# Where two blocks of tokens are scaled and stored: a hybrid decoder layer on one core

## The chip, the cores and the metric

One core of a Trainium2 chip runs the whole kernel. The metric is the device time of one execution in microseconds; the profile is one further execution, recorded instruction by instruction on the same program. TensorE is called PE, VectorE DVE, ScalarE ACT, GpSimd POOL and SyncE SP in all tables.

## The reference, cut to what matters

One decoder layer over 4096 new tokens and 64 sample tokens. Only its first half is concerned here: the normalised tokens times one projection, whose columns are then given to a convolution, a windowed attention and a cross-attention.

```python
def _rmsnorm(x, g):
    xf = x.astype(jnp.float32)
    r = lax.rsqrt(jnp.mean(xf * xf, axis=-1, keepdims=True) + RMS_EPS)
    return (xf * r).astype(x.dtype) * g

def _layer(x, ...):
    h = _rmsnorm(x, g_pre)          # 1024 features
    z = h @ w_in                    # 22 column tiles of 128
    cb, cc, ch, cg, q, k, v, ag, mq, mg = _split_cols(z)
    ...
    y = jnp.concatenate([out_a, out_b, out_c], axis=-1) @ w_out
    return x + _rmsnorm(y, g_post), new_conv, new_k, new_v
```

## The kernel before, in words

**Tiles and phases.** The 4160 tokens are cut into 8 blocks of 520; a block is four tiles `B11`, `B21`, `B12`, `B22` of 128 partitions x 4 x 260 (feature half by token half). The 22 column tiles of the weight are done in three phases over all blocks: in the names of the code and here phase 0, 1 and 2 (the short title's "phase 1" and "phase 2" are phases 0 and 1). Every operand is split into a high and a low part (`split`, line 273 on ACT and 274 on DVE), and a product is three matmuls per k (`product`, line 283). Most blocks use Strassen's seven products (`PRODUCTS`); the operands T1 to T4 are differences of the four tiles (`t_sum`, line 266). One product on four column tiles is a "step" of 48 matmuls.

**The two plain blocks.** Phase 0 begins with blocks 0 and 1 done with eight plain products each (`plain_block`), since the Strassen sums of the weights are not there yet. What is done beside each step is written out by hand in `plain_jobs` and `plain_loads`. All of phase 0 is issued in program order on every engine (`manual_schedule`); phases 1 and 2 are ordered by the scheduler. In the plain blocks the row factors of the norm are not applied to x but afterwards to the result z (`z_rows`, line 527).

**Row factors.** `row_load` loads 104 token rows (tile `nat`, two buffers, line 207) on SP; `row_step` squares and sums them on ACT (line 218). After five of these POOL computes the factors (lines 222 and 223) and stores them to the DRAM tensor `rowd` (line 224). `row_queue` puts the collected row loads on SP and, two calls later, the load that spreads `rowd` over all partitions (tile `rb`, two buffers, line 234). SP works its queue in order, so whatever waits there holds up all that stands behind it.

**Tokens for phases 1 and 2.** In phase 0 each x tile is loaded from `in_xt` (line 188), multiplied by the gain on ACT (line 246) and by its row factor on DVE (line 254; line 252 for block 0, with the gain), and stored to the DRAM tensor `hd` through POOL's queue (line 127). For the plain blocks the split needs only the gain, or no more than x itself in block 0 (line 491), so their scaled copies are made for later phases alone. Phase 1 loads x from `hd` (line 442).

**Other names.** `temp` is a ring of 6 buffers in phase 0; the results of a finished block (`finish`: `th`, `v`, `zh`, `kl_`) are made in it, and each of its buffers is free once the store of its last user has landed. `flush` hands the collected stores to the queue at the next step. `o_kn`, `o_kc`, `o_vc` (lines 1129 to 1131), the loads of `us` (line 366) and of `gmem` (line 626) are copies with no fixed place, which the scheduler has put early in SP's queue, between the loads of the plain blocks.

Of the kernel before, what the change touches and what calls it, by code (L numbers as in the profile page):

```python
# [8 lines left out]
F32 = mybir.dt.float32  # L9
# [3 lines left out]
ALU = mybir.AluOpType  # L13
AX = mybir.AxisListType

P = 128
# [35 lines left out]
def hybrid_layer(ctx: ExitStack, tc: tile.TileContext, a: dict):  # L52
# [38 lines left out]

    def open_phase(ph):
        nonlocal tp, zp, natp, pa2, pa1
        tp = own.enter_context(tc.tile_pool(name=f"t{ph}", bufs=(6, 9, 4)[ph]))
        if ph == 0:
            natp = own.enter_context(tc.tile_pool(name="nat", bufs=2))
        zp = own.enter_context(tc.tile_pool(name=f"z{ph}", bufs=(5, 7, 3)[ph]))
        if ph != 1:

            psa.close()  # L100
            pa2 = psa.enter_context(tc.tile_pool(name=f"pa{ph}", bufs=2, space=bass.MemoryType.PSUM))
            if ph == 2:
                pa1 = psa.enter_context(tc.tile_pool(name="pa1", bufs=1, space=bass.MemoryType.PSUM))
# [76 lines left out]
    def x_load(b, o):  # L180

        kh, g0 = int(o[1]) - 1, (2 * b + int(o[2]) - 1) * HW
        t = hxp.tile([P, KH, HW], F32, tag="hx", name=f"x{b}{o}")
        g = g0
        while g < g0 + HW:
            src, off, n = (a["xt0"], g, 320) if g < 320 else (a["xt"][(g - 320) // 384], (g - 320) % 384, 384)
            w = min(n - off, g0 + HW - g)
            DMA.dma_start(t[:, :, g - g0 : g - g0 + w], src[:, KH * kh : KH * kh + KH, off : off + w])
            g += w
        return t  # L190

    RG = 104

    rows = []
    nat, sq = {}, [0]

    row_loads, row_spreads = [], {}

    def row_load(j):
        if j < 5 * NBLK:  # L200
# [26 lines left out]
    def row_queue():  # L227

        for j in row_loads:
            row_load(j)  # L230
        row_loads.clear()
        for b in [b for b, n in row_spreads.items() if n == 1]:
            rows.append(natp.tile([P, 2 * HW], F32, tag="rb", name=f"rb{b}"))
            DMA.dma_start(rows[b], rowd[b].partition_broadcast(P))
        for b in list(row_spreads):
            row_spreads[b] -= 1
            if row_spreads[b] == 0:
                del row_spreads[b]
# [8 lines left out]

    def scale(x, b, o):
        rb = rows[b][:, HW * (int(o[2]) - 1) : HW * int(o[2])]
        if b == 0:  # L250
            for k in range(KH):
                V.scalar_tensor_tensor(x[:, k], x[:, k], gain_of(o, k), rb, op0=ALU.mult, op1=ALU.mult)
        else:
            V.tensor_tensor(x, x, rb.unsqueeze(1).to_broadcast([P, KH, HW]), op=ALU.mult)
        store(hd[b][o], x)

    def t_sum(ph, b, o):

# [98 lines left out]
    def finish_conv(b, ct, zc, zh, zg, zb):  # L357
        zc, zh, zg, zb = (flat(z) for z in (zc, zh, zg, zb))
        n = 2 * HW
        ns = NS if b == 0 else 0  # L360
        m = n - ns
        V.scalar_tensor_tensor(zg, zb, 0.5, zg, op0=ALU.mult, op1=ALU.mult)
        ub = temp(f"ub{b}_{ct}")[:, : 2 + m]
        if ns:
            us = tiny.tile([P, NB, 10], F32, tag="us", name=f"us{ct}", bufs=2)
            DMA.dma_start(us[:, :, 0:2], a["convst"][ct])
            V.memset(ub[:, 0:2], 0.0)
            V.tensor_tensor(us[:, :, 2:10], zc[:, :ns].rearrange("p (b t) -> p b t", b=NB),
                            zh[:, :ns].rearrange("p (b t) -> p b t", b=NB), op=ALU.mult)
# [61 lines left out]
    def h_split(i):  # L431
        if i < len(steps):
            ph, b, p = steps[i]
            o = PRODUCTS[p][1]
            hs[i] = split(xs[ph, b][o], f"{ph}_{b}{o}")

    def x_of(ph, b, o):
        if ph == 0:
            t = x_load(b, o)
        else:  # L440
            t = hxp.tile([P, KH, HW], F32, tag="hx", name=f"x{ph}_{b}{o}")
            DMA.dma_start(t, hd[b][o])
        xs.setdefault((ph, b), {})[o] = t

    def x_gain(b, o):
        gain(xs[0, b][o], o)

    def x_scale(b, o):
        scale(xs[0, b][o], b, o)

    def x_ready(ph, b, o):
        if ph == 0:
            x_gain(b, o)
            x_scale(b, o)

    def next_block(ph, b, p):

# [7 lines left out]
            jobs = [load(o) for o in jobs]  # L465
        if p < 3:
            jobs.append(lambda: t_sum(ph, b, f"T{p + 2}"))
        if ph == 0 and (1 <= p < 6 or (b, p) == (PLAIN_BLOCKS, 0)):
            jobs.append(row_step)
        if nph < 2:  # L470
            jobs += [ready(o) for o in {4: "B11", 5: "B21 B12", 6: "B22"}.get(p, "").split()]
            if p == 6:
                jobs.append(lambda: t_sum(nph, nb, "T1"))
        return jobs

# [3 lines left out]

    def x_split(b, o):
        x = xs[0, b][o]
        if b > 0:
            h0[b, o] = split(x, f"0_{b}{o}")
            return
        h0[b, o] = hi, lo = [hp.tile([P, KH, HW], F32R, tag=n, name=f"{n}0_{b}{o}") for n in ("hi", "lo")]
        for k in range(KH):
            g = gain_of(o, k)  # L490
# [38 lines left out]

    def plain_jobs(b, s):  # L530

        gains = lambda b, *os: [lambda o=o: x_gain(b, o) for o in os]
        scales = lambda b, *os: [lambda o=o: x_scale(b, o) for o in os]
        parts = lambda b, o: [lambda: x_split(b, o)]
        fill = lambda o: [lambda q=q: first_fill(o, q) for q in range(4)]
        sums = lambda q, k: [lambda: first_sums(q, k)]
# [9 lines left out]
            (0, 5): lambda: [*sums(1, 0), *gains(1, "B11"), *sums(1, 1), *fills(1, "S2"), *row, *fills(1, "S3")],  # L546
            (0, 6): lambda: [*parts(1, "B11"), *fills(1, "S1", "S4"), *row, *sums(3, 0), *gains(1, "B21")],
            (0, 7): lambda: [*fills(3, "S2", "S3"), *row, *fills(3, "S1")],
            (1, 0): lambda: [*parts(1, "B21"), *scales(0, "B11", "B21"), *row, *z_rows(0, 1), *row],
            (1, 1): lambda: [*z_rows(0, 0), *done(0, 1), *row, *row],  # L550
            (1, 2): lambda: [*scales(0, "B12", "B22"), *done(0, 0), *row, *gains(1, "B12"), *row],
            (1, 3): lambda: [*parts(1, "B12"), *sums(2, 0), *gains(1, "B22"), *row],
            (1, 4): lambda: [*sums(2, 1), *fills(2, "S2"), *scales(1, "B11"), *row, *scales(1, "B21")],
            (1, 5): lambda: [*parts(1, "B22"), *gains(2, "B11"), *fills(2, "S3"), *row, *fills(2, "S1", "S4"), *gains(2, "B21")],
            (1, 6): lambda: [*scales(1, "B12", "B22"), *row, *scales(2, "B11", "B21")],
            (1, 7): lambda: [lambda: h_split(0), *gains(2, "B12"), *scales(2, "B12"), lambda: t_sum(0, 2, "T1"), *row,
                             *gains(2, "B22"), *scales(2, "B22"), *z_rows(1, 1)],
        }[b, s]()

    def plain_loads(b, s):  # L560
        for o in {(0, 0): ["A22"], (0, 1): ["A12"]}.get((b, s), ()):
            first_w(o)
        if (b, s) == (0, 0):
            row_load(0)
            row_load(1)
        row_queue()
        for nb, o in {(0, 1): [(0, "B12")], (0, 2): [(0, "B22")], (0, 4): [(1, "B11")], (0, 5): [(1, "B21")],
                      (1, 2): [(1, "B12"), (1, "B22")], (1, 4): [(2, "B11"), (2, "B21")],
                      (1, 6): [(2, "B12"), (2, "B22")]}.get((b, s), ()):
            x_of(0, nb, o)  # L570

    def plain_block(b):
        banks, zz[b] = {}, [[None, None], [None, None]]
# [45 lines left out]
    def third_start():  # L619
# [3 lines left out]
        third["pre"] = pre_stack.enter_context(tc.tile_pool(name="pre", bufs=1, side="right"))  # L623
        third["mem"] = mem_stack.enter_context(tc.tile_pool(name="mem", bufs=3, side="right"))
        third["ps"] = psa.enter_context(tc.tile_pool(name="psm", bufs=2, space=bass.MemoryType.PSUM))
        DMA.dma_start(gmem, a["gmem"])

    def mem_load(k):
        xm = third["mem"].tile([P, 256], F32, tag="xm", name=f"xm{k}")
# [70 lines left out]
    def input_projection():  # L700
        raws = {}
        for i, (ph, b, p) in enumerate(steps):
# [14 lines left out]
            h_load(i + 3)  # L717
            h_split(i + 1)
            jobs = list(pending.pop(i, ()))
            if ph == 0:  # L720
                row_queue()
            if ph < 2:
                jobs += next_block(ph, b, p)
            if ph == 2:
# [336 lines left out]
    def sample_window(sp):  # L1061
# [61 lines left out]
        for j in range(4):  # L1123
            for kvh in range(2):
# [1 line left out]
                c0 = (kvh * 4 + j) * 8  # L1126
                V.scalar_tensor_tensor(mix_s[r, 4 + j, :].rearrange("p (b t) -> p b t", b=NB), o3[r, :, c0 : c0 + 8], 0.5,
                                       zs[r, 6 + j, :].rearrange("p (b t) -> p b t", b=NB), op0=ALU.mult, op1=ALU.mult)
        DMA.dma_start(a["o_kn"], zs[:, 4:6, :])
        tc.keep_in_program_order(DMA.dma_start(a["o_kc"], a["cwk_nat"]))  # L1130
        tc.keep_in_program_order(DMA.dma_start(a["o_vc"], a["cwv_nat"]))
        yield
# [257 lines left out]
```

## Time and profile before

| | us |
|---|---|
| median of three runs | 1694.85 (1692.13 to 1697.65) |
| the profiled execution, whole | 1707.98 |
| its span | 1706.3 |
| PE busy / DVE busy / ACT busy / POOL busy | 1594.1 / 1183.9 / 784.2 / 358.5 |
| phase 0 on PE, first matmul to the first of phase 1 | 8.87 to 404.39 |

The profiled execution is 13.1 us longer than the median run. Busy time of PE is not time at full speed: the clock that it is granted falls to 0.5 in places, and a mean of 0.965 is recorded over the span. Instruction lists give start, duration, engine, line, operation with output and inputs, and in brackets how long the engine had stood idle and what released it. The lists of waits give total, number and longest.

### The profile page before, as it was taken

How to read it: one execution, taken by the hardware profiler on the slowest of the kernel's cores; microseconds unless marked ns; L12 is line 12 of the kernel's file. 1: busy time of each engine (PE TensorE's matmuls, PEld its weight loads, DVE VectorE, ACT ScalarE, POOL GpSimd, SP SyncE). 2: the span in 40 equal slices, each digit the busy share in tenths (PEclk: the TensorE clock that was granted, in tenths of full speed). 3: DMA queues.
4: the chain of work that ended last, by engine and by line, in shares of the span. 5: the costliest groups of instructions: out<-in, count | busy, mean ns of one | idle time of the engine just before them, and what ended most of it. 6: DMA issues, size and time to landing. Idle time of an engine off the chain costs nothing.

```text
span 1706.3 us, 29560 instructions
## 1 busy us (share of the span) xinstructions
PE 1594.1 (93%) x11073; PEld 1409.8 (83%) x11073; DVE 1183.9 (69%) x2113; ACT 784.2 (46%) x2000; POOL 358.5 (21%) x595
## 2 busy tenths in 40 slices
PE   7856999998999999979999975999999999999998
PEld 7856999998999999979999963677777777777766
DVE  6736777788788777965666656677677766767743
ACT  6544555555222222434443435555555555555521
POOL 0312222221000000000000014444443344333320
PEclk9977999999999999999999987999999999999989
DMA  7798899967565333669775769676677776666151
GB/s 215 148 261 214 213 243 251 252 235 272 135 214 176 127 114 115 217 171 272 252 249 197 255 176 193 126 151 141 140 143 156 156 160 133 136 151 135 50 182 62
DMA packets 170228, 306.69 MB, mean 180 GB/s; under 512 B 29030, under 2 KB 98406, under 8 KB 170054
## 3 DMA queue, kind: packets, MB, share of 16 engines
q1 hardware_dynamic: 123157, 226.21, 43.3%
q0 software_dynamic: 46928, 78.59, 23.7%
q8 instruction: 88, 1.44, 0.4%
q14 instruction: 55, 0.44, 0.1%
HBM read 196.54 MB, written 109.19 MB: 179 GB/s over the span
## 4 chain that ended last, share of the span: by engine, by line
PE 48%; DVE 19%; DMA 10%; issue 9%; ACT 8%; POOL 5%; SPq 0%; ACTq 0%; POOLq 0%; DVEq 0%
PE c L283 36%; PE y L1213 6%; ACT sm L954 5%; DVE sm L960 3%; DMA md<-th 2%; DVE sm L944 2%; DVE wmx L946 2%; DMA wor<-in_w_out 2%; POOL xp L909 2%; DVE yn L1220 1%; PE wt L964 1%; PE xs L901 1%; DVE xr L1231 1%; DVE mix L928 1%; ACT xp L905 1%
## 5 line engine op out<-in xcount | busy, mean ns | idle before, releaser
L1213 PE MATMUL y<-wo,mh 128*128 128x512 f32 (+1 forms) x1072 | 351.8, 392 | 1.4 <-DVE mh L1190 1.4
L290 DVE TENSOR_TENSOR z<-c,z 128x520 f32<-128x520 f32 (+1 forms) x308 | 195.0, 646 | 105.5 <-PE c L283 99.9
L1213 PEld LDWEIGHTS y<-wo,mh 128*128 128x128 f32 x1072 | 201.1, 189 | 42.1 <-issue 2.8
L1213 PE MATMUL y<-wo,ml 128*128 128x512 f32 (+1 forms) x520 | 202.8, 390 | 0.0
L954 ACT ACTIVATE sm<-sm,wnm 128x128 f32<-128x128 f32 x256 | 99.9, 391 | 76.1 <-DVE wnm L948 76.1
L1213 PEld LDWEIGHTS y<-wo,ml 128*128 128x128 f32 x520 | 98.4, 189 | 15.3
L941 PE MATMUL ws<-kst,q 128*128 128x256 f32 x512 | 82.3, 303 | 8.6 <-ACT sm L943 5.9
L971 POOL TENSOR_SCALAR_AFFINE_SELECT wpv<-wpt 128x512 f32<-128x512 f32 x62 | 40.2, 648 | 225.9 <-ACT wpt L966 225.2
L941 PEld LDWEIGHTS ws<-kst,q 128*128 128x128 f32 x512 | 68.8, 198 | 11.1 <-ACT sm L943 6.4
L902 DVE TENSOR_REDUCE xmx<-xs 128x2 f32<-128x512 f32 x64 | 44.2, 691 | 43.3 <-PE xs L901 43.3
L905 ACT ACTIVATE xp<-xs,xnm 128x256 f32<-128x256 f32 x128 | 59.4, 470 | 27.4 <-DVE xnm L903 27.1
L909 POOL TENSOR_SCALAR xp<-xp,xrd 128x256 f32<-128x256 f32 x128 | 63.3, 502 | 37.4 <-DVE xrd L906 34.6
L943 ACT COPY sm<-ws 128x256 f32<-128x256 f32 x128 | 44.6, 372 | 56.8 <-PE ws L941 54.0
L1221 ACT ACTIVATE y<-y 128x512 f32<-128x512 f32 (+1 forms) x66 | 38.8, 587 | 66.5 <-DVE yn L1220 66.5
L843 POOL MEMSET kst<- 128x512 f32 x1 | 0.5, 527 | 324.2 <-DVE cacc L389 324.2
L1220 DVE TENSOR_TENSOR yn<-y,gpost 128x512 f32<-128x512 f32 (+1 forms) x66 | 45.1, 684 | 31.5 <-PE y L1213 31.4
L1231 DVE SCALAR_TENSOR_TENSOR xr<-yn,yst,xr 128x1024 f32<-128x1024 f32 (+2 forms) x34 | 42.5, 1253 | 30.2 <-POOL yst L1227 30.2
L964 PEld LDWEIGHTS wt<-ident,sm 128*128 128x128 f32 x256 | 28.6, 147 | 40.2 <-issue 18.3
L901 PE MATMUL xs<-mk,q 128*128 128x256 f32 x256 | 47.3, 308 | 11.4 <-ACT xp L905 8.4
L960 DVE TENSOR_TENSOR sm<-sm,wrd 128x512 f32<-128x512 f32 x64 | 55.0, 860 | 2.1
L344 DVE SCALAR_TENSOR_TENSOR th<-th,z 128x520 f32<-128x520 f32 x48 | 32.8, 695 | 33.1 <-ACT th L343 33.1
L914 PEld LDWEIGHTS xt<-ident,xp 128*128 128x128 f32 x256 | 29.7, 142 | 31.2 <-PE wo L827 12.2
(931 smaller groups left out, 5147.3 us busy)
## 6 DMA issues: line engine op xcount, KB each, us to landing
q<-qd POOLq DMA_DIRECT2D x64, 384.0 KB, 8.7
mix<-md SPq DMA_DIRECT2D x16, 1024.0 KB
xr<-in_x_p SPq DMA_DIRECT2D x32, 512.0 KB
nat<-in_x_p SPq DMA_DIRECT2D x39, 416.0 KB
o_yp<-xr SPq DMA_DIRECT2D x31, 512.0 KB
md<-th POOLq DMA_DIRECT2D x48, 260.0 KB, 8.3
qd<-zh SPq DMA_DIRECT2D x48, 260.0 KB
qd<-z SPq DMA_DIRECT2D x48, 260.0 KB
```

What stands on the lines that cost most here:

```text
L283: TE.matmul(bank[:, :HW], l, r, start=first and i == 0, stop=last and i == 3 * KH - 1)
L290: add = lambda dst, other: V.tensor_tensor(dst, c, other, op=ALU.add)
L901: TE.matmul(s[:, i, :], q[:, i * P : i * P + P], third["mk"][:, part, h, :], start=part == 0, stop=part == 1)
L905: S.activation(p[:, i, :], s[:, i, :], AF.Exp, bias=nm[:, i : i + 1], scale=SCALE, accum_out=den[:, i : i + 1])
L909: G.tensor_scalar(p[:, i, :], p[:, i, :], rd[:, i : i + 1], 0.5, op0=ALU.mult, op1=ALU.mult)
L941: TE.matmul(s3[:, hh, :], self.q[:, 4 + 2 * (2 * half + hh) + kvh, i * P : i * P + P], self.kst[:, 2 * kvh + part, i * P : i * P + 2 * P], ...
L954: S.activation(sm[:, hh, :], sm[:, hh, :], AF.Exp, bias=nm[:, hh : hh + 1], scale=SCALE, accum_out=den[:, hh : hh + 1])
L960: V.tensor_tensor(sm, sm, rd.unsqueeze(2).to_broadcast([P, 4, P]), op=ALU.mult)
L964: TE.transpose(t[:, hh * P : (hh + 1) * P], sm[:, hh, :], ident)
L1213: TE.matmul(acc, self.hl[l][:, k], wo[k][:, r, c0:c1], start=j == 0, stop=j == passes * KT - 1)
L1220: V.tensor_tensor(yn[:m, c0:c1], acc[:m], gpost[:m, c0:c1], op=ALU.mult)
L1231: V.scalar_tensor_tensor(self.xr[:m, cs], yn[:m, cs], st[:m, 3:4], self.xr[:m, cs], op0=ALU.mult, op1=ALU.add)
```

## The change

- Blocks 0 and 1 are split with the gain straight from x; in phase 0 they get no scaled copy and no store to `hd`.
- Phase 1 loads the x tiles of blocks 0 and 1 from `in_xt` again, with their `rb` again, and does gain, scale and store (`B12`, which no later phase reads, is not stored) while the previous block runs.
- The x tiles of blocks 1 and 2 are loaded some steps earlier, and in each step in front of the row loads; in the Strassen blocks `row_queue` is a job behind the step's x load.
- The row steps and gains are set to other steps, `temp` in phase 0 has 7 buffers for 6, and the loads of `us` and `gmem` and the store `o_kn` keep their program order, so that they and `o_kc` and `o_vc` come late.

```diff
-        tp = own.enter_context(tc.tile_pool(name=f"t{ph}", bufs=(6, 9, 4)[ph]))
+        tp = own.enter_context(tc.tile_pool(name=f"t{ph}", bufs=(7, 9, 4)[ph]))
...
+    def rows_load(b, again=False):
+        rows[b] = (temp(f"rb{b}")[:, : 2 * HW] if again else natp.tile([P, 2 * HW], F32, tag="rb", name=f"rb{b}"))
+        DMA.dma_start(rows[b], rowd[b].partition_broadcast(P))
...
     def scale(x, b, o):
         rb = rows[b][:, HW * (int(o[2]) - 1) : HW * int(o[2])]
-        if b == 0:
-            for k in range(KH):
-                V.scalar_tensor_tensor(x[:, k], x[:, k], gain_of(o, k), rb, op0=ALU.mult, op1=ALU.mult)
-        else:
-            V.tensor_tensor(x, x, rb.unsqueeze(1).to_broadcast([P, KH, HW]), op=ALU.mult)
-        store(hd[b][o], x)
+        V.tensor_tensor(x, x, rb.unsqueeze(1).to_broadcast([P, KH, HW]), op=ALU.mult)
+        if b >= PLAIN_BLOCKS or o != "B12":
+            store(hd[b][o], x)
...
     def x_of(ph, b, o):
-        if ph == 0:
+        if ph == 0 or b < PLAIN_BLOCKS:
             t = x_load(b, o)
...
     def x_ready(ph, b, o):
-        if ph == 0:
-            x_gain(b, o)
-            x_scale(b, o)
+        x_gain(ph, b, o)      # both: only if ph == 0 or b < PLAIN_BLOCKS
+        x_scale(ph, b, o)
...   (next_block)
-        if ph == 0 and (1 <= p < 6 or (b, p) == (PLAIN_BLOCKS, 0)):
-            jobs.append(row_step)
+        if ph == 0:
+            jobs.append(row_queue)
+            if 1 <= p < 6:
+                jobs.append(row_step)
+        if p == 1 and nph == 1 and nb < PLAIN_BLOCKS:
+            jobs.append(lambda: rows_load(nb, nb > 0))
...   (x_split)
-        if b > 0:
-            h0[b, o] = split(x, f"0_{b}{o}")
-            return
...   (plain_jobs, block 1)
-            (1, 0): lambda: [*parts(1, "B21"), *scales(0, "B11", "B21"), *row, *z_rows(0, 1), *row],
+            (1, 0): lambda: [*parts(1, "B21"), *row, *z_rows(0, 1), *row],
             (1, 1): lambda: [*z_rows(0, 0), *done(0, 1), *row, *row],
-            (1, 2): lambda: [*scales(0, "B12", "B22"), *done(0, 0), *row, *gains(1, "B12"), *row],
-            (1, 3): lambda: [*parts(1, "B12"), *sums(2, 0), *gains(1, "B22"), *row],
+            (1, 2): lambda: [*row, *done(0, 0)],
+            (1, 3): lambda: [*parts(1, "B12"), *sums(2, 0), *row],
...   (plain_loads)
+        for nb, o in {(0, 1): [(0, "B12")], (0, 2): [(0, "B22")], (0, 3): [(1, "B11")], (0, 4): [(1, "B21")],
+                      (0, 6): [(1, "B12")], (0, 7): [(1, "B22")], (1, 1): [(2, "B11")], (1, 2): [(2, "B21")],
+                      (1, 4): [(2, "B12")], (1, 5): [(2, "B22")]}.get((b, s), ()):
+            x_of(0, nb, o)
         row_queue()
-        for nb, o in {(0, 1): [(0, "B12")], (0, 2): [(0, "B22")], (0, 4): [(1, "B11")], (0, 5): [(1, "B21")],
-                      (1, 2): [(1, "B12"), (1, "B22")], (1, 4): [(2, "B11"), (2, "B21")],
-                      (1, 6): [(2, "B12"), (2, "B22")]}.get((b, s), ()):
-            x_of(0, nb, o)
...
-            DMA.dma_start(us[:, :, 0:2], a["convst"][ct])
+            tc.keep_in_program_order(DMA.dma_start(us[:, :, 0:2], a["convst"][ct]))
...
-        DMA.dma_start(gmem, a["gmem"])
+        tc.keep_in_program_order(DMA.dma_start(gmem, a["gmem"]))
...
-        DMA.dma_start(a["o_kn"], zs[:, 4:6, :])
+        tc.keep_in_program_order(DMA.dma_start(a["o_kn"], zs[:, 4:6, :]))
```

More of the change, by code (lines that the diff above doesn't have):

```diff
@@ L182, in x_load @@
         kh, g0 = int(o[1]) - 1, (2 * b + int(o[2]) - 1) * HW
-        t = hxp.tile([P, KH, HW], F32, tag="hx", name=f"x{b}{o}")
+        t = hxp.tile([P, KH, HW], F32, tag="hx", name=f"xl{b}{o}")
         g = g0
@@ L192, in hybrid_layer @@
     RG = 104
-    rows = []
+    rows = {}
     nat, sq = {}, [0]
     row_loads, row_spreads = [], {}
+    def rows_load(b, again=False):
+        rows[b] = (temp(f"rb{b}")[:, : 2 * HW] if again else natp.tile([P, 2 * HW], F32, tag="rb", name=f"rb{b}"))
+        DMA.dma_start(rows[b], rowd[b].partition_broadcast(P))
     def row_load(j):
@@ L232, in row_queue @@
         for b in [b for b, n in row_spreads.items() if n == 1]:
-            rows.append(natp.tile([P, 2 * HW], F32, tag="rb", name=f"rb{b}"))
-            DMA.dma_start(rows[b], rowd[b].partition_broadcast(P))
+            rows_load(b)
         for b in list(row_spreads):
@@ L443, in x_of, with x_gain, x_scale @@
         xs.setdefault((ph, b), {})[o] = t
[L445 to L449, printed above, removed]
+    def x_gain(ph, b, o):
+        if ph == 0 or b < PLAIN_BLOCKS:
+            gain(xs[ph, b][o], o)
+    def x_scale(ph, b, o):
+        if ph == 0 or b < PLAIN_BLOCKS:
+            scale(xs[ph, b][o], b, o)
     def x_ready(ph, b, o):
-        if ph == 0:
-            x_gain(b, o)
-            x_scale(b, o)
+        x_gain(ph, b, o)
+        x_scale(ph, b, o)
     def next_block(ph, b, p):
@@ L530, in plain_jobs @@
     def plain_jobs(b, s):
-        gains = lambda b, *os: [lambda o=o: x_gain(b, o) for o in os]
-        scales = lambda b, *os: [lambda o=o: x_scale(b, o) for o in os]
+        gains = lambda b, *os: [lambda o=o: x_gain(0, b, o) for o in os]
+        scales = lambda b, *os: [lambda o=o: x_scale(0, b, o) for o in os]
         parts = lambda b, o: [lambda: x_split(b, o)]
@@ L545, in plain_jobs @@
             (0, 4): lambda: [*parts(0, "B22"), *fills(0, "S3", "S1"), *row, *fills(0, "S4"), *row],
-            (0, 5): lambda: [*sums(1, 0), *gains(1, "B11"), *sums(1, 1), *fills(1, "S2"), *row, *fills(1, "S3")],
-            (0, 6): lambda: [*parts(1, "B11"), *fills(1, "S1", "S4"), *row, *sums(3, 0), *gains(1, "B21")],
-            (0, 7): lambda: [*fills(3, "S2", "S3"), *row, *fills(3, "S1")],
-            (1, 0): lambda: [*parts(1, "B21"), *scales(0, "B11", "B21"), *row, *z_rows(0, 1), *row],
+            (0, 5): lambda: [*sums(1, 0), *row, *sums(1, 1), *fills(1, "S2"), *row, *fills(1, "S3")],
+            (0, 6): lambda: [*parts(1, "B11"), *fills(1, "S1", "S4"), *row, *sums(3, 0)],
+            (0, 7): lambda: [*fills(3, "S2", "S3"), *row, *fills(3, "S1"), *row],
+            (1, 0): lambda: [*parts(1, "B21"), *row, *z_rows(0, 1), *row],
             (1, 1): lambda: [*z_rows(0, 0), *done(0, 1), *row, *row],
-            (1, 2): lambda: [*scales(0, "B12", "B22"), *done(0, 0), *row, *gains(1, "B12"), *row],
-            (1, 3): lambda: [*parts(1, "B12"), *sums(2, 0), *gains(1, "B22"), *row],
[L553 to L557, printed above, removed]
+            (1, 2): lambda: [*row, *done(0, 0)],
+            (1, 3): lambda: [*parts(1, "B12"), *sums(2, 0), *row],
+            (1, 4): lambda: [*sums(2, 1), *fills(2, "S2"), *gains(2, "B11"), *row],
+            (1, 5): lambda: [*parts(1, "B22"), *fills(2, "S3", "S1", "S4"), *gains(2, "B21")],
+            (1, 6): lambda: [*row, *gains(2, "B12"), *scales(2, "B11", "B21"), *row],
+            (1, 7): lambda: [lambda: h_split(0), *gains(2, "B22"), *scales(2, "B12"), lambda: t_sum(0, 2, "T1"), *row,
+                             *scales(2, "B22"), *z_rows(1, 1)],
         }[b, s]()
@@ L719, in input_projection @@
             jobs = list(pending.pop(i, ()))
-            if ph == 0:
-                row_queue()
             if ph < 2:
```

## The prediction

> **What bounds the kernel now.** I read the chain of waits of PE first, then the timeline for the first matmul of each block, then the queues behind the longest wait. PE's starts:
>
> ```profile
> 56.88 0.28 PE L283 MATMUL c<-hi_1B,w_0A 128*128 128x260 f32 x1
> 129.26 0.58 PE L283 MATMUL c<-hi_2B,w_0A 128*128 128x260 f32 x1 [3.36 <-ACT hi_2B L273]
> 189.67 0.28 PE L283 MATMUL c<-hi_3B,w_0A 128*128 128x260 f32 x1
> 234.19 0.28 PE L283 MATMUL c<-hi_4B,w_0A 128*128 128x260 f32 x1
> 280.55 0.28 PE L283 MATMUL c<-hi_5B,w_0A 128*128 128x260 f32 x1
> 322.24 0.28 PE L283 MATMUL c<-hi_6B,w_0A 128*128 128x260 f32 x1
> 364.15 0.28 PE L283 MATMUL c<-hi_7B,w_0A 128*128 128x260 f32 x1
> 404.39 0.28 PE L283 MATMUL c<-hi_0B,w_0A 128*128 128x260 f32 x1
> 451.74 0.28 PE L283 MATMUL c<-hi_1B,w_0A 128*128 128x260 f32 x1
> ```
>
> Block 7 has no stall: 40.24 us for seven steps, 5.75 a step. A plain block of eight steps is then 46.0. So PE loses 26.4 us in block 1 (72.4), 20.2 in block 2, 4.3, 6.1, 1.5 and 1.7 in blocks 3 to 6: 60 us in phase 0, and 7.1 in the first block of phase 1. Phase 0 is held up by what feeds PE, mostly in two blocks. The waits between 75 and 330:
>
> ```profile
> ACT th L343 <- DMA md<-th: 25.9, 5, 9.8
> PE c L283 <- ACT hi_1B L273: 19.6, 1, 19.6
> ```
>
> Behind the 19.6 stands ACT, and behind ACT, SP's queue:
>
> ```profile
> 83.21 0.64 ACT L343 ACTIVATE th<-z 128x520 f32<-128x520 f32 x1 [4.19 <-DMA md<-th]
> 95.89 1.72 ACT L246 ACTIVATE x1B<-x1B,gpre 128x260 f32<-128x260 f32 x4 [8.54 <-DMA x1B<-in_xt]
> ```
> ```profile
> 55.26 24.25 SPq L207 DMA_DIRECT2D nat<-in_x_p  x6
> 79.60 0.81 SPq L234 DMA_DIRECT2D rb<-rowd  x1
> 81.41 1.70 SPq L188 DMA_DIRECT2D x1B<-in_xt  x2
> ```
>
> PE ran out at 79.7. The load that it needed left SP only at 81.4, behind six row loads and an `rb` that waited for `rowd` (issued at 70.80); it then shared the DMA with everything that had piled up and landed near 95.9. PE's clock, 1.00 up to 80, is granted at 0.50 from 85.0 to 105. Block 2 repeats it: x scaled late because `rb` was late (10.2 us on DVE), then `th` 9.8 us late because the ring of 6 was full, and PE waits 8.6 us at once for T3. In blocks 3 to 6 the ring costs ACT 3.3 to 4.6 us each.
>
> **The change part by part.**
>
> *Block 1.* The loads of its third and fourth tile now stand six steps, 34 us, before their use and ahead of `rb` 1 on SP: the 8.54 is gone. 16 scalings of block 0 leave DVE (2 x 3.28 us), and 8 stores of 520 KB leave POOL's queue, four of them among the `md` stores that ACT waited for (4.19). `o_kn` with its 4.2 us wait on SP goes too. Alone, without the 8.54, ACT is free at 87.4; hi is made in pieces straight from x (4 x 0.43), so PE would go on at about 88: a stall of 8.5. What now stands ahead of hi on ACT: `th` 3, moved from 68.5 only to about 68 because the split waits for one more row square; three row squares, 1.25 each, the last with its load behind `rb` 1. `rowd` 1 leaves near 62.5 and lands near 71.5; that row is in at 75. ACT then has 6 us of `th`, `zs`, `zh` and copies: hi at about 82.5, a stall of 3 to 4. The new ring use at `wa2A` (four temps, waiting for stores that land near 90) holds the next lo to about 94, where PE needs it at 95. Bounds for what block 1 still loses: 2 (no stall but the last waits) and 16 (`rb` 1 lands as late as the slowest `rowd` below, and the clock drops). I take 8, nearer the low end because the chain of rows is known and only its last link varies: gain 18.
>
> A row weighed against a page: the write of `rowd` took 9.7, 8.8 and 14.7 us from its start (45.10, 70.80, 105.48) to the `rb` that waits for it (54.82, 79.60, 120.22). The Trainium skill, "DMA: Bandwidth & Descriptors", section "Anatomy of one DMA — SWDGE (gpsimd) path", gives about 2 us fixed for such a transfer; by that `rb` 1 could go at 65, the 3 to 4 us stall would shrink to about 1, and the forecast would be some 3 us lower. These three rows disagree, and the sum goes by them.
>
> *Block 2.* Its x tiles and `rb` 2 come before need (x by 10 to 20 us; `rb` 2 near 92, first used near 97): the 3.4, the 2.6 and the half clock behind them go, about 8. `th` 3 is stored at once, since POOL no longer stands at a row factor (148.58 for a `th` made at 140.6); with 7 buffers the wait moves from `th` 6 to `zh`, and falls from 9.8 to 2 to 4, most of which the step before T3 hides. Left over between 0 and 14 (as now, less the x part); I take 4, by the slack of one step: gain 16.
>
> *Blocks 3 to 6.* The seventh buffer moves the ring's wait by one tile, that is to a step 5.75 us later, more than the 3.3 to 4.6 now waited; x loads go ahead of rows. 13.6 lost now, 0 to 13.6 later. DMA was busy 0.89 to 0.97 of the time from 200 to 350, so I take 5: gain 8.6.
>
> *Block 7 and the first blocks of phase 1, where the work goes.* The 4 x 4 gains cost ACT 6.9 us a block, and the 4 scalings DVE 4 x 1.24 = 5.0, twice. DVE is back to back from 390.6 to 412:
>
> ```profile
> 408.66 1.24 DVE L274 TENSOR_TENSOR lo_0B<-x_0B,hi_0B 128x1040 fp32r<-128x1040 f32 x1
> ```
>
> This lo is needed at 410.1. Behind 5.0 us of scalings and one more weight split (0.69) it starts at 414.3: PE stalls about 5. But PE stalls 4.5 there now, one step later, for ACT's copy of z at 419.9 (ACT stood 6.4 for weights whose buffer the ring held; the seventh frees the first of them). The two overlap: net +3, at worst +9 (both in full), at best -1. In block 1 of phase 1 DVE's gaps (3.0 and 2.2 near 426, some 3 up to 450) take the second 5.0; the loads of `us` now issue a few us before use (1.65 to 2.2 us each, behind a store that waits for DVE): 0 to 2, I take 1. x is read in pieces of 240 to 1040 bytes for 4160: 0.1 to 0.7 us more a load, all a step or more ahead. `o_kc`, `o_vc`, `o_kn` at the end: 4.4 us of SP while DMA is at 0.17; `gmem` is loaded seven steps ahead: 0. The cover for both is an idle SP; without it they cost those 4.4 and 1.4.
>
> **The sum.** 18 + 16 + 8.6 - 3 - 1 = 39 off the profiled execution's 1708.0. That run is 13 us above the median, and what a slower DMA adds sits where DMA is waited for, so a part of the 13 is stall that the median run lacks; I count a third: 35 off the median, **1660**.
>
> **The rivals.**
>
> *The row chain moves in (slower).* Rows' loads now stand behind x loads, and ACT runs its squares in order ahead of hi and of the copies that free PE's banks. SP already waits 141.3 us in 32 pieces for squares and 81.9 for `rowd`:
>
> ```profile
> SPq L207 <- ACT nat L218: 141.3, 32, 16.2
> SPq L234 <- DMA rowd<-r: 81.9, 6, 20.7
> ```
>
> If each of the 20 squares in the plain blocks waits as long for its row as the worst so far (3.38 us on ACT), that is 68 us: 1660 + 68 = 1728, less what falls in PE's slack. It turns the sign from about 2 us a square on. Against it: ACT waited 4.9 in all for rows so far. Chance 0.08.
>
> *The new bound is DVE at the seam.* 5.7 us of lag in block 7 that the short phase-1 blocks never work off, and a clock drop with each wait: +9 and +6, and blocks 3 to 6 gain nothing: 18 + 16 - 15 = 19 off, 1676 by the median. For it: DVE idles under 2 us in 380 to 415. Chance 0.17.
>
> *DMA fills whatever is freed.* The x loads change place, but SP still stands at the same squares (the third tile comes behind two rows of the step before), and block 1 keeps its stall: 1690 to 1695. Against it: those squares run at 42 to 47, 30 us before use. Chance 0.05.
>
> *Everything goes.* All 60 us, no cost at the seam: 1640 or less. Chance 0.07.
>
> A residual stall and the clock: PE idle from 79.7 was at half clock by 85.0, and took until 105, 5.4 us of work, to come back; after 154.3 it fell already at 156.7. The Trainium skill, "TensorE: Matmul & The Clock Gate", section "Part 1: The HAM clock gate", says one idle window of some 3.4 us halves it, with a free-running window. By that, whether my 3 to 4 us in block 1 cost another 1.7 to 3.4 is chance; both are inside the 8.
>
> **How the numbers follow.** Forecast as summed 0.63, rivals 0.08, 0.17, 0.05, 0.07. The range leaves out the row chain and the far ends: 1641 to 1686. A measurement of this kernel tells about 0.3%, 5 us, from no change. Faster: forecast, seam, everything and part of the DMA case, 0.88; within 0.3%: 0.03; slower: 0.09.
>
> **What would show it.** Right: in the profile after, block 1 (first `hi_1B` to first `hi_2B`) near 54, block 2 near 44, blocks 3 to 6 near 41.5, phase 0 ending near 362; no ACT wait for x in block 1; one DVE wait of PE at the first steps of phase 1, and that block 50 long rather than 47.4. Wrong: ACT waits for `nat` of 2 us and more in a row, or PE waiting on lo in phase 1 for over 10 us in all.

## The result and the profile after

| | before | after |
|---|---|---|
| median of the paired runs, us | 1697.24 | 1683.42 (1678.22 to 1686.39) |
| ratio, 95% interval | | 0.9924 (0.9906 to 0.9943) |
| profiled execution / its span | 1707.98 / 1706.3 | 1686.34 / 1684.6 |

The median is 13.8 us lower, where 35 were forecast; the two spans differ by 21.7 us, where 39 were forecast. PE's starts by block in the profile after (with the one long wait):

```profile
57.12 0.28 PE L283 MATMUL c<-hi_1B,w_0A 128*128 128x260 f32 x1
...
99.94 0.58 PE L283 MATMUL c<-hi_1B,w_0A 128*128 128x260 f32 x1 [19.68 <-ACT hi_1B L493]
...
125.76 0.28 PE L283 MATMUL c<-hi_2B,w_0A 128*128 128x260 f32 x1
169.67 0.28 PE L283 MATMUL c<-hi_3B,w_0A 128*128 128x260 f32 x1
210.34 0.28 PE L283 MATMUL c<-hi_4B,w_0A 128*128 128x260 f32 x1
254.61 0.28 PE L283 MATMUL c<-hi_5B,w_0A 128*128 128x260 f32 x1
297.02 0.28 PE L283 MATMUL c<-hi_6B,w_0A 128*128 128x260 f32 x1
337.27 0.28 PE L283 MATMUL c<-hi_7B,w_0A 128*128 128x260 f32 x1
377.52 0.28 PE L283 MATMUL c<-hi_0B,w_0A 128*128 128x260 f32 x1
430.88 0.28 PE L283 MATMUL c<-hi_1B,w_0A 128*128 128x260 f32 x1
```

Differences of these starts give the ledger; the last column is the sum of the prediction.

| stretch | before | after | gain | forecast |
|---|---|---|---|---|
| block 1 | 72.4 | 68.6 | 3.8 | 18 |
| block 2 | 60.4 | 43.9 | 16.5 | 16 |
| blocks 3 to 6 | 174.5 | 167.6 | 6.9 | 8.6 |
| first block of phase 1 | 47.4 | 53.4 | -6.0 | -3 |
| all else in the span | | | 0.5 | -1 |

"All else" is what the difference of the spans leaves: the time before block 1, block 7 and everything behind the first block of phase 1. Block 2 and blocks 3 to 6 came near the forecast. Block 1 kept a stall of 19.7 us, and the seam (the first block of phase 1) lost double the 3 us. The list of waits from 75 to 330, as it was shown for before (total, number, longest):

```profile
ACT nat L222 <- DMA nat<-in_x_p: 36.6, 13, 6.9
...
PE c L283 <- ACT hi_1B L493: 19.7, 1, 19.7
...
ACT th L343 <- DMA md<-th: 5.3, 4, 3.8
```

The ring's wait for `th`, 25.9 before, is down to 5.3. In its place ACT now waits 36.6 for token rows. ACT's queue in block 1:

```profile
66.32 1.06 ACT L222 ACTIVATE nat<-nat 104x1024 f32<-104x1024 f32 x1 [5.45 <-DMA nat<-in_x_p]
...
91.55 1.06 ACT L222 ACTIVATE nat<-nat 104x1024 f32<-104x1024 f32 x1 [6.94 <-DMA nat<-in_x_p]
...
99.38 1.72 ACT L493 ACTIVATE hi_1B<-xl1B,gpre 128x260 fp32r<-128x260 f32 x4
```

No ACT wait for x is left in block 1, as the prediction said. But the split that PE needs at 80 (the making of `hi_1B`) stands behind the squares, and the last of these gets its row at 91.55, not at 75. SP's queue shows when the loads were issued:

```profile
57.65 10.15 SPq L211 DMA_DIRECT2D nat<-in_x_p  x3
...
79.65 0.36 SPq L201 DMA_DIRECT2D rb<-rowd  x1
...
82.21 10.83 SPq L211 DMA_DIRECT2D nat<-in_x_p  x3
```

The first loads of these two groups were issued at 57.65 and 82.21, and their squares began at 66.32 and 91.55: 8.7 and 9.3 us for 426 KB each. Both went out just behind the `rb` that had waited for `rowd` (56.73 and 79.65), into what had piled up while `rowd` was written. PE's waits at the seam, 362 to 432 (before, one of 4.5 us for z):

```profile
PE c L283 <- ACT z L292: 3.0, 1, 3.0
PE c L283 <- DVE z L290: 2.4, 1, 2.4
PE c L283 <- DVE lo_0B L274: 1.4, 1, 1.4
PE c L283 <- DVE lo_0T L274: 1.3, 2, 0.9
```

**Why the rows are late.** The packets of the trace (the pieces in which the DMA moves a transfer) point to it. The trace records the time of each. A 4096-byte packet of SP's queue (row loads) and a 4160-byte packet of POOL's queue (its stores, those to `md` and `hd` among them) took, among those that began between 40 and 300 us, on average:

| | 3 to 10 us after a store of `rowd` begins to be issued | at other times |
|---|---|---|
| before, 4096 / 4160 | 584 / 935 ns | 235 / 194 ns |
| after, 4096 / 4160 | 525 / 779 ns | 229 / 202 ns |

In one such stretch, with block 0's `rowd` issued at 45.83 and its `rb` released at 56.73, the DMA moved 25 GB/s (the columns are the stretch, its length, the busy time of PE, PEld, DVE, ACT and POOL with the number of instructions, PE's granted clock, the DMA's busy share and GB/s):

```profile
52.00:56.00 4.00, 4.00 (x35) 4.00 (x35) 3.64 (x7) 2.63 (x6) 0.00 (x0) 1.00 0.44 25
```

`rowd` is written from 104 partitions x 5 values; the five of a partition go to places 416 bytes apart, so the store has 520 pieces of 4 bytes. Two theories were to be told apart. **A**: order alone. SP's `rb` waits for `rowd`, row loads stand behind it, and on ACT the squares stand ahead of the split. **B**: while the 4-byte pieces are written, every other transfer crawls, so the rows (and the stores that free the ring) land late.

### The profile page after: what moved, and what is told of

It is laid out like the page before. It is cut to its first block, busy times and chain, and to the rows that moved or that the text cites. A ratio compares the mean times of both kernels' runs of the same rounds, so it can differ in the third digit from the quotient of the medians.

```text
span 1684.6 us, 29573 instructions
## 1 busy us (share of the span) xinstructions
PE 1585.2 (94%) x11073; PEld 1401.4 (83%) x11073; DVE 1182.1 (70%) x2113; ACT 791.2 (47%) x2028; POOL 349.7 (21%) x590
## 4 chain that ended last, share of the span: by engine, by line
PE 43%; DVE 17%; ACT 7%; issue 3%; DMA 3%; POOL 3%; ACTq 0%; SPq 0%; POOLq 0%; DVEq 0%
PE c L283 30%; PE y L1213 6%; ACT sm L954 5%; DVE sm L960 3%; DVE sm L944 2%; DVE wmx L946 2%; DMA wor<-in_w_out 2%; POOL xp L909 2%; PE wt L964 1%; DVE yn L1220 1%; PE xs L901 1%; PE wo L827 1%; DVE xr L1231 1%; DVE mix L928 1%; ACT xp L905 1%
## 5 line engine op out<-in xcount | busy, mean ns | idle before, releaser
L222 ACT ACTIVATE nat<-nat 104x1024 f32<-104x1024 f32 x40 | 42.3, 1058 | 48.2 <-DMA nat<-in_x_p 48.0
L964 PEld LDWEIGHTS wt<-ident,sm 128*128 128x128 f32 x256 | 28.0, 144 | 40.3 <-issue 18.1
L960 DVE TENSOR_TENSOR sm<-sm,wrd 128x512 f32<-128x512 f32 x64 | 54.9, 858 | 2.0
```

What stands on the lines that cost most here:

```text
L960: V.tensor_tensor(sm, sm, rd.unsqueeze(2).to_broadcast([P, 4, P]), op=ALU.mult)
L964: TE.transpose(t[:, hh * P : (hh + 1) * P], sm[:, hh, :], ident)
```

## The experiments

All ratios are to the kernel before, run alongside on the same chip; a difference between two runs is read from their ratios. "Block n" is the distance between PE's starts in the one profiled execution of a run. Such a distance varies: in the five profiles of experiments 6 (second run) and 7, whose phase 0 has the same code, block 1 took 52.3 to 54.6 us.

**1. `rb` without its wait, and no `rowd` at all.** Change: in phase 0 `rb` reads an input; then, in both phases, and the store goes too.

```diff
-        DMA.dma_start(rows[b], rowd[b].partition_broadcast(P))
+        DMA.dma_start(rows[b], (rowd[b] if again else a["gpost"][: 2 * HW]).partition_broadcast(P))   # e1
+        DMA.dma_start(rows[b], a["gpost"][: 2 * HW].partition_broadcast(P))                          # e2
-            G.dma_start(rowd[b].rearrange("(i p) -> p i", p=RG), r[:RG, 0:5])                         # e2
```

> The changed kernel, but in phase 0 the six loads of rb read an input instead of rowd (so the row factors of phase 0 are wrong); rowd is still written in its 4-byte pieces, and SP never waits for it. Theory A (SP's order: rb waits for rowd, and the row loads stand behind it, so the squares on ACT come late): the four row waits of block 1 (5.5, 1.6, 2.3, 6.9 us) fall to under 4 us in all, block 1 goes from 68.6 to about 55, and the kernel gains 10 us or more against the change. Theory B (the 4-byte writes of rowd slow every transfer that is under way with them, and the rows are late for that): only the first wait shrinks, by the 1 to 3 us for which SP stood behind rb; block 1 stays at 64 to 69, and the time is within 5 us of the change's.

Measured: 1690.72, ratio 0.9944 (0.9926 to 0.9961), where the change has 0.9924: no gain on it. Block 1 took 67.9, and ACT's waits for rows from 55 to 126 were 15.7 us, against 17.3:

```profile
ACT nat L222 <- DMA nat<-in_x_p: 15.7, 6, 5.8
```

So SP's wait for `rowd` is not what makes the rows late.

> As the run before, and rowd is not written at all: no wait for it and no 4-byte pieces (all row factors wrong). Theory A: the same time as the run before within 3 us, since SP's wait was gone already. Theory B: 4-KB packets take some 230 ns throughout instead of 900 to 1500 while rowd is written; rows land 3 to 4 us after their issue instead of 9; PE's 19.7 us wait falls below 8, block 1 to 50 to 57, and the kernel gains 12 us or more against the run before. A third possibility, that the rows are late because the DMA simply has too many bytes to move there (x, md and rows): the packets stay slow, and block 1 stays above 64 in both.

Measured: 1673.52, 0.9855 (0.9829 to 0.9880). Block 1 took 56.0, PE's wait for the split 8.1, blocks 3 to 7 40.2 or 40.3 each, and the waits for rows were 6.8:

```profile
ACT nat L222 <- DMA nat<-in_x_p: 6.8, 3, 4.4
```

In phase 0 the two runs differ only in the store of 2 KB per block, and it is worth 0.9% (15 us). Theory B holds, and the number of bytes is not the limit. The 8.1 us that are left are taken up in experiment 6.

**2. The same store in 20-byte pieces.** Nothing is left out: the rows of a block are dealt out so that partition p holds rows 5p to 5p+4. The row loads change with it: each takes every fifth row, still 4096 bytes per partition, and those of block 0 (not shown) are two loads each.

```diff
-            G.dma_start(rowd[b].rearrange("(i p) -> p i", p=RG), r[:RG, 0:5])
+            G.dma_start(rowd[b].rearrange("(p i) -> p i", i=5), r[:RG, 0:5])
-                DMA.dma_start(t[:RG], a["x_p"][g : g + RG, :])
+                DMA.dma_start(t[:RG], a["x_p"][g : g + 2 * HW, :].rearrange("(p i) d -> p i d", i=5)[:, i])
```

> The changed kernel with the rows of a block dealt out to the partitions five at a time (partition p holds rows 5p to 5p+4), so that rowd is written in 104 pieces of 20 bytes instead of 520 of 4; everything else is the same and nothing is left out. Theory B: the time from the store's issue to rb falls from about 10 us to 3 to 5, the slow stretches with it, and the kernel gains most of what the run without rowd gains, 8 us or more against the change. Theory A: rb comes earlier by the same 5 to 7 us, the wait for the first late row shrinks with it, and the gain is that of the run with rb from an input. No change if a write's time does not go by its pieces.

Measured: 1675.48, 0.9855 (0.9822 to 0.9888), the ratio of the run without the store; block 1 59.7, block 2 42.7, blocks 3 to 7 40.2 or 40.3. The time from issue to landing of `rowd` (least, median, most) in the change, where the trace has it for four of the eight stores, and then with 20-byte pieces, for all eight:

```profile
DMA to landing us min/median/max: 10.9/12.1/13.1
```
```profile
DMA to landing us min/median/max: 1.8/5.7/6.4
```

And the stretch 74 to 80 in both, columns as above; a `rowd` had been issued at 69.35 and 66.89. The third line is the stretch with 20-byte pieces in which that store was itself under way:

```profile
74.00:80.00 6.00, 6.00 (x53) 6.00 (x51) 2.22 (x4) 2.61 (x8) 2.23 (x4) 1.00 0.59 67
```
```profile
74.00:80.00 6.00, 6.00 (x52) 6.00 (x51) 0.70 (x1) 3.84 (x9) 1.63 (x3) 1.00 0.94 280
68.00:74.00 6.00, 6.00 (x53) 6.00 (x52) 5.07 (x6) 2.76 (x8) 0.60 (x1) 1.00 0.94 219
```

That is 67 GB/s against 280, with row loads and `md` stores pending in both (part of the 280 is x, which SP could issue sooner there). Near a `rowd` the two kinds of packet now take 271 and 188 ns, elsewhere 253 and 179: the slow stretches are gone. The Trainium skill, "DMA: Bandwidth & Descriptors", section "Rules for kernel authors", says that a last dimension that is not contiguous lowers to one descriptor per element, and to rearrange so that it is. The two runs agree with this advice, and give a price that the rule does not: 6 us of landing time, and the slowing of the transfers beside it.

**3. The same 4-byte pieces from SP's queue.**

```diff
-            G.dma_start(rowd[b].rearrange("(i p) -> p i", p=RG), r[:RG, 0:5])
+            DMA.dma_start(rowd[b].rearrange("(i p) -> p i", p=RG), r[:RG, 0:5])
```

> The changed kernel with rowd written from SP's queue instead of POOL's, in the same 520 pieces of 4 bytes. If the pieces are what slows the other transfers, packets of 4 KB still take 700 to 1500 ns beside it, block 1 stays at 64 to 72 and the time at 1680 to 1690 (SP stands some 2 us more for POOL's results). If it is POOL's queue, the slow stretches go as with the 20-byte pieces, and the time comes to 1673 to 1678.

Measured: 1702.30, 1.0003 (0.9981 to 1.0024), slower than the 1680 to 1690 expected; block 1 took 71.6, within its range. The 4096-byte packets near a `rowd` take 625 ns, elsewhere 283. So it is the pieces and not POOL's queue. On SP they are worse placed, since the queue's own row loads come right behind them:

```profile
ACT nat L222 <- DMA nat<-in_x_p: 29.5, 4, 13.2
```

The trace records the store from SP's queue as packets of 4 bytes, but from POOL's queue as 16 packets of 160 bytes, so there its pieces are known from the instruction (5 x 104 elements of 4 bytes), not from packets. The Trainium skill, "DMA: Bandwidth & Descriptors", section "Issuing engines are not separate DMA queues", says that starting transfers from several engines saves only the time to issue them. The run agrees: 1.0003 against the 0.9924 with the store on POOL.

**4. The seventh buffer, taken out of the change, and alone.**

```diff
-        tp = own.enter_context(tc.tile_pool(name=f"t{ph}", bufs=(7, 9, 4)[ph]))   # e4; e5 is the reverse, on before
+        tp = own.enter_context(tc.tile_pool(name=f"t{ph}", bufs=(6, 9, 4)[ph]))
```

> The changed kernel with the ring of temporary tiles back at 6. By the prediction's steps the seventh buffer is what took the stalls from blocks 3 to 6 (174.5 to 167.6 us here) and, with POOL's queue relieved, the wait of 9.8 us for th in block 2 (60.4 to 43.9): blocks 3 to 6 return to 172 to 175, block 2 to 46 to 52, and the kernel is 8 to 15 us slower than the change. Rival (the stores that left phase 0 and the x loads ahead of rows did it): blocks 2 to 6 within 3 us of the change, and the time within 5.

Measured: 1703.70, 1.0033 (1.0010 to 1.0057): slower than before, and 1.1% (18 us) behind the change, where 8 to 15 us were expected. Block 2 took 49.2, blocks 3 to 6 177.6. ACT's wait for the ring is back, from 75 to 340:

```profile
ACT th L343 <- DMA md<-th: 23.5, 5, 6.9
```

> The kernel before with the ring of temporary tiles at 7 and nothing else. With the ring at 6 the change was 0.3% slower than before, with 7 it is 0.8% faster. If the seventh buffer alone carries the gain (the moved scalings, stores and loads being worth nothing together), this run comes to 1678 to 1688, with block 1 still at 72, block 2 at 50 to 55 and blocks 3 to 6 at 41 to 42 each. If the gain needs the move too, because the ring's wait in block 2 and the x loads of block 1 both stay, it comes to 1690 or more.

Measured: 1693.19, 0.9949 (0.9922 to 0.9977). Blocks 3 to 6 took 40.2, 40.3, 41.8 and 41.2, but block 1 69.7 and block 2 61.5. The buffer alone brings 0.5%, and the move without it costs 0.3%. In blocks 3 to 6 the buffer does it. In block 2 the move does most (60.4 to 49.2), and the buffer helps only on top of it (to 43.9).

**5. The 20-byte pieces in the kernel before, with the ring at 6 and at 7.** The edit is that of experiment 2 on the old kernel, then with that of 4.

> The kernel before with its row factors written in 20-byte pieces. If the 4-byte writes slow all transfers and hold rb, they cost the kernel before as well: its x load of block 1 stood behind rb (issued 79.6, with rowd from 70.8) and block 2 had rb and th late; block 1 72 to 60 to 66, block 2 60 to 50 to 56, the time 10 to 18 us less than before. If they matter only where row loads stand on ACT's path (the change), the time stays within 5 us of before.

Measured: 1673.12, 0.9837 (0.9800 to 0.9874): 28 us off, twice the change itself, and more than the 10 to 18 expected. Block 1 took 63.5, block 2 50.3, and blocks 3 to 6 40.2 or 40.3 each with six buffers. The ring's wait from 75 to 330, 25.9 us before:

```profile
ACT th L345 <- DMA md<-th: 5.6, 3, 3.5
```

The `md` stores issued between 60 and 340 us, for whose landing the ring waits, landed after 9.3 us on median in the kernel before and after 4.2 here. So the ring was full because the `md` stores were slowed beside `rowd`; the seventh buffer of the change only covers that.

> The kernel before with the 20-byte pieces and with the ring at 7: what the change would have stood against had rowd been cheap. With the ring at 6 it took 1673, blocks 3 to 6 already at 40.2 each, so the seventh buffer has nothing left there: 1668 to 1674, with at most 3 to 5 us in block 2 (50.3). Then the move of the scalings, with the split ahead (1666), is worth 2 to 8 us, since it gains 11 in blocks 1 and 2 beyond this and pays 6 to 8 back in the first block of phase 1. If the ring still carries most, it comes below 1666.

Measured: 1673.50, 0.9820 (0.9793 to 0.9847): the buffer is worth 0.2% now, within the intervals. The change with 20-byte pieces (0.9855) is no faster than this, and the intervals overlap, so with `rowd` cheap no gain of the move is shown. Its parts can be seen: the moved scalings gain about 5 us in blocks 1 and 2 (102.4 against 107.4) and lose 7.8 at the seam (54.9 against 47.2).

**6. ACT's order in block 1.**

```diff
-            (1, 1): lambda: [*z_rows(0, 0), *done(0, 1), *row, *row],
-            (1, 2): lambda: [*row, *done(0, 0)],
-            (1, 3): lambda: [*parts(1, "B12"), *sums(2, 0), *row],
+            (1, 1): lambda: [*z_rows(0, 0), *done(0, 1), *row],
+            (1, 2): lambda: [*parts(1, "B12"), *done(0, 0), *row],
+            (1, 3): lambda: [*row, *sums(2, 0), *row],
```

> The changed kernel with the order of block 1's work on ACT changed alone: the split of its third tile stands at the head of step (1, 2), ahead of two row squares and of the finishing of block 0, and those two squares go one step later. Theory A', that what PE waits for is ACT's order (squares that wait for their rows stand ahead of hi_1B): PE's 19.7 us wait falls to 3 to 8 us although the rows land as late as before, block 1 goes from 68.6 to 52 to 58, the kernel gains 8 to 14 us on the change. If the rows only take the next thing away (ACT's copies that free PE's banks, behind the same squares), block 1 stays above 62 with the wait on z instead of hi.

Measured: 1683.58, 0.9897 (0.9861 to 0.9933). The split comes 17.5 us sooner, and the last wait ahead of it is one of 2 us:

```profile
80.84 1.06 ACT L222 ACTIVATE nat<-nat 104x1024 f32<-104x1024 f32 x1 [2.05 <-DMA nat<-in_x_p]
...
81.89 1.70 ACT L493 ACTIVATE hi_1B<-xl1B,gpre 128x260 fp32r<-128x260 f32 x4
```

PE's longest wait falls from 19.7 to 4.3. But block 1 takes 61.5, not 52 to 58, since each of its steps from the fourth on takes 7.8 to 10.2 us, and block 2 gives 5 back (49.0). The gain on the change is 0.3%, within the intervals, and half or less of what was expected. ACT still waits for two rows behind the split (1.8 and 2.8 us): the rows are still late, and hold the next thing.

> Both cures together: rowd in 20-byte pieces and the split of the third tile ahead. If they are two causes of one wait (late rows, and hi behind them) the gains do not add: block 1 48 to 52 against 59.7 with the 20-byte pieces alone, so 6 to 10 us less than that run, about 1667. If ACT's order did nothing by itself, the time is that of the run with the 20-byte pieces, 1675.

Measured: 1665.97, **0.9792 (0.9756 to 0.9829)**, block 1 52.3, block 2 42.7, phase 0 ended at 354.6. Of the kernels that leave nothing out this is one of the two fastest, 2.1% or 36 us under the one before, and the time is that expected. It is 0.3% ahead of the kernel before with 20-byte pieces and seven buffers (0.9820), within the intervals. PE's wait for the split:

```profile
PE c L285 <- ACT hi_1B L495: 3.4, 1, 3.4
```

**7. What the first block of phase 1 pays for.** All on the kernel with both cures (20-byte pieces, and the split ahead), where this block is 55.4 long. In the seven profiles whose phase 1 has the code of the change it took 52.9 to 56.6, so differences of 2 or 3 us between two profiles say little.

```diff
-        V.tensor_tensor(x, x, rb.unsqueeze(1).to_broadcast([P, KH, HW]), op=ALU.mult)     # e10: in phase 1 left out; e12: on G
-                    {0: "B11", 3: "B21", 4: "B12", 5: "B22"}.get(p, "").split()
+                    {2 if b == 0 else 0: "B11", 3: "B21", 4: "B12", 5: "B22"}.get(p, "").split()   # e11
-        if b >= PLAIN_BLOCKS or o != "B12":
+        if b >= PLAIN_BLOCKS:                                                             # e13
             store(hd[b][o], x)
```

> Both cures (20-byte pieces, split ahead), and in phase 1 the 8 scalings of blocks 0 and 1 on DVE are left out (the loads, gains and stores stay; the outputs of phase 1 are wrong by that). The prediction's step: DVE's 5 us of scalings make lo late in the first block of phase 1; then that block falls from 55.4 to 48 to 51. The rival: ACT waits 7.8 us for a weight whose ring buffer comes free late, amid 520-KB stores of scaled x and the loads of block 1's x; then it stays at 53 to 56.

Measured: 1665.16, 0.9770 (0.9731 to 0.9809), the block 53.0, just in the range that the rival gave. DVE's scalings are worth at most some 2.4 us of it, no more than profiles vary, and the total does not differ from that with both cures. PE's waits for DVE in the block fall from 5.0 to 1.8 us, but its wait for ACT's z grows from 5.2 to 8.1, so the one had covered the other:

```profile
PE c L286 <- ACT z L295: 8.1, 1, 8.1
```

> Both cures, and the first tile of block 1's x in phase 1 is loaded two steps later (it is used four steps after its load now), so that 520 KB leave the stretch in which the weights' loads are awaited. If bytes in that stretch make the weight late: ACT's wait for it falls from 7.8 to 5 or less and the first block of phase 1 from 55.4 to 51 to 54. If the ring's release does (a store issued only after DVE's work): no change, 55 to 56.

Measured: 1664.87, 0.9775 (0.9740 to 0.9810), the block 56.6: no gain there, though ACT's longest wait for a weight (`wr_2S`) fell from 7.8 to 5.3. The total does not differ from that with both cures.

> Both cures, and the 8 scalings of blocks 0 and 1 in phase 1 run on POOL instead of DVE. No row of the trace shows such an operation on POOL: an estimate from DVE's 1.24 us is 2 to 5 us each. By the prediction's step (DVE's time is what the block lacks) the first block of phase 1 falls to 49 to 52, if POOL takes under 3 us; beyond 4 us each, the md stores queued behind them on POOL come later and the block takes 57 or more. By the rival (ring and bytes) 55 or more either way.

Measured: 1673.09, 0.9819 (0.9787 to 0.9850), the block 61.1 and block 7 44.3. POOL takes 2.4 to 3.0 us for six of the scalings, 3.4 and 5.3 for the others, mostly under the 3 that were to suffice, yet the block got longer instead of falling to 49 to 52. So taking the scalings off DVE does not bring back what the block lacks; the rival's 55 or more held. PE waits 6.4 us for `lo_0B`, which points to the longer chain from gain to scale to `lo`; that was not tested by itself.

> Both cures, and the six stores of scaled x of blocks 0 and 1 in phase 1 are left out (phase 2 reads another block's in their place, so its outputs are wrong there). If these 520-KB stores, which stand on POOL among the md stores and in the DMA among the loads of weights, are what the first block of phase 1 pays for: it falls from 55.4 to 47 to 50 and the kernel gains 5 us or more on 1666. If its cost is the order of the work on ACT and DVE there (gains and scalings ahead of what PE waits for): 53 to 56, no gain beyond 3 us.

Measured: 1657.22, 0.9746 (0.9721 to 0.9772), 0.5% under both cures, with intervals that just overlap; the block took 49.6, below all seven profiles named above. (Phase 2 loads another block's tiles in place of those not stored.) PE's waits from 340 to 406:

```profile
PE c L285 <- DVE z L292: 2.3, 1, 2.3
PE c L285 <- DVE lo_0B L276: 1.4, 1, 1.4
PE c L285 <- ACT z L294: 0.7, 1, 0.7
```

The long wait for z (5.2 us with both cures) is down to 0.7. The stores of scaled x cost some 5.9 us of this block, most of the 8 that it has over the 47.4 of before. This is one profile of the kernel with both cures; that the stores cost as much in the change itself was not measured. Whether they cost by their bytes or by their place in POOL's queue was not separated.

## Why the prediction was right or wrong

- **Block 1, +18: wrong, and the cause of the miss.** The first half held: the wait for x went. The step that failed is the arrival of the last row ahead of the split: "that row is in at 75" and "the chain of rows is known and only its last link varies". Its square began at 91.55, and more than one link was late: `rowd` 1 left at 69.35 instead of near 62.5, behind a square whose row came late as well. The left-over was put at 8, between 2 and 16, and measured 22.6 (68.6 less 46.0), beyond both ends: 19.7 of it is PE's wait, and 2.8 the step after it, which took 8.6 us for 5.75 under a granted clock of 0.50. The working gave a row load the time of an undisturbed one and let `rowd` only delay `rb`; the runs showed that the store slows the transfers that are under way with it. Without the store block 1 took 56.0; with 20-byte pieces and the split ahead of the late squares it took 52.3, near the 54 that was forecast. The evidence stood in the profile of before: a store of 2 KB that took 8.8 to 14.7 us was used as the price of a wait, and nothing was asked of what the DMA did meanwhile.
- **The rival "the row chain moves in"** described what happened in block 1 (five waits, 17.3 us, the longest 6.9) and was given 0.08 because it was priced as slower. Its sign, ACT waits for `nat` of 2 us and more, was there. It replaced the gain rather than reversing it, since the kernel before had lost the same 20 us in the same place. It should have had a version of the size of the removed stall. The rival "DMA fills whatever is freed" (0.05, 1690 to 1695) had block 1 keep its stall, but for x, for which ACT no longer waited.
- **Block 2, +16: right** (16.5). The ring and the move were both needed, as its working had it: without the buffer it is 49.2, without the move 61.5. The cause beneath was not seen: 20-byte pieces alone bring the block from 60.4 to 50.3 in the kernel before.
- **Blocks 3 to 6, +8.6: right in size** (6.9), and the buffer is shown to be what did it. That it "moves the ring's wait by one tile" explains the cover; the cause beneath, slow `md` stores beside `rowd`, was not seen.
- **Seam, -3 (bounds -9 to 1): mis-sized**, 6.0 lost. DVE's delay came as worked out: `lo_0B` began 9.2 us after the block's start, against 4.3, and PE's waits for DVE add up to 5.1. But the overlap was mis-judged: of the 4.5 us for ACT's z, 3.0 stayed beside them. The waits then grew by 3.6; the rest of the 6.0 was not taken apart. The working took eight 520-KB stores off block 1 and never put the six that come back into its sum for phase 1; on the kernel with both cures they are some 5.9 us, against at most some 2.4 for the scalings, on which the whole term rested. The rival "DVE at the seam" was 7 us off in time (1676); it had blocks 3 to 6 gain nothing, and they gained 6.9.
- **`us` loads and the end, -1**: all else is +0.5; a difference of this size is not told apart from none by one profile of each kernel.
- **Profile to median**: 4 us less gain was allowed, 7.9 less measured (21.7 against 13.8): right in direction.
- **A reading.** After the idle that began at 154.3 the granted clock fell at 156.2, not at 156.7; no term of the sum hangs on it.
- **The whole.** Direction and range held (1683.4 in 1641 to 1686), but near the upper end: the gain was less than half of the forecast's 35. That blocks 2 to 6 came near their terms is in part luck, since the cover was right and the cause beneath it was not seen.

## What to carry to other kernels

When a small transfer takes many times what its bytes would need, look at what the others do meanwhile: count its contiguous pieces before adding buffers or moving loads, for a store of 2 KB was worth more here than the whole change. A wait that is removed from an in-order queue of work is worth only the distance to the next late thing in it (here 3.8 us where 18 were forecast), so price that thing's arrival from loads taken at the same moment. And carry each store that leaves one stage into the sum of the stage where it returns.

## What the runs showed of the hardware

A store of 520 pieces of 4 bytes took 9.3 to 13.1 us to land (before and after, where the trace has it) and held other packets to some 2 to 5 times their usual time, with the store on POOL's queue (584 against 235 and 935 against 194 ns before) as on SP's (625 against 283); 104 pieces of 20 bytes took 1.8 to 6.4 us and had almost no effect on the others (271 against 253 and 188 against 179). Beside the former the DMA moved 25 and 67 GB/s in two stretches, beside the latter 219 in one. Why a piece costs so much is not shown.
